# Output projection of a hybrid attention block: float16 hi/lo pairs with a scale in place of float32r pairs

## The chip, the core and the metric

The kernel runs on one core of a Trainium2 chip. The core has a matrix engine (TensorE; its weight loads are shown apart), three engines for elementwise work and reductions (VectorE, ScalarE, GpSimd), and a queue of its own for issuing transfers (SyncE); all run at the same time and wait for each other through semaphores. The time of a run is in microseconds on the device. The profile is of one execution and covers the span from its first to its last instruction.

## The reference

One layer of an encoder block over 1024 tokens of width 1024. One projection `h = x @ W_in` gives the columns of two groups of heads and of their gates; group A is neighbourhood attention over a 64 x 16 grid with a learned bias, group B is windowed grouped-query attention with rotary positions and a sink. What bears on the change is the end:

```
mixed = concat([y_a * silu(z_a), y_b * silu(z_b)], axis=-1)      # 1024 tokens x 1024
y     = mixed @ W_out                                            # 1024 x 1024
out   = LayerNorm(ALPHA * x + y, gain, bias)                     # ALPHA = 2 ** 0.25
```

All inputs and outputs are float32. A product of two float32 matrices is formed in this kernel from pairs: each operand is split into a part `hi` in a shorter type and the rest `lo`, and three products are added: hi x hi, hi x lo, lo x hi.

## The kernel before

All products are built of 128 x 128 stationary tiles and moving tiles of up to 512 columns. The stages follow one another, and overlap.

1. **V projection** (L430, to 61.7 us): x and the V columns of W_in in float32r pairs. Beside it the scale of x is found (`x_max`, `x_scale`), and x is loaded a second time and split into scaled float16 pairs (`x16_part`).
2. **Six first projections** (61.7 to 124.3 us): `project` (L334) for the first `NPRO = 6` names of `ORDER`: gate tiles zb0, z0, zb1, the keys and first queries of group B, and gate z1. A name is a tile of 128 columns of W_in and takes 48 matmuls of 512 columns in L355: two token halves, eight k-tiles, three products. W_in is split into float16 pairs after scaling with a power of two: `w_scan` or `sum_w` sums the absolute values of a tile, `w_scale` forms the total over the partitions with a matmul against `ones` (L207) and derives the scale. For the first six names a tile has a scale of its own; the other 15 share one, for which `sum_w` reads them all once in this stage, tile i at step 14 + 14 i; eight of them stay in SBUF, seven are loaded again later.
3. **Attention** (124.3 to about 374 us): 128 units. Each has a score product (L709, L710), row maximum and exponential, a split of the probabilities with a DMA transpose, the product with V (L774), and a transposition back (L794) with which the gate is multiplied in. Between the units' matmuls the other 15 projections are fed in, by a table of times (`FILL_AT`), and after them the first 60 output matmuls (`out_head`).
4. **Output projection** (`out_mms`, L899; 350.9 to 445.7 us): per token tile t and column half a, eight k-tiles e of three products each. `m_split` and `m_queue` make float32r pairs of the gated tiles (`mh`, `ml`), `wo_split` makes those of the 16 half tiles of W_out. Each finished half goes to `residual` (VectorE: ALPHA x + y, with statistics), and each finished token tile to `norm` and out.

What sets the order of the work: in stages 1 and 2 the instructions stand in each engine's queue as the program emits them (`tc.manual_schedule`). In stage 2 a counter `ran` goes up by one per projection matmul (`run_to`, L364), and work listed with `at(c, ...)` is emitted when it reaches c: this text calls c the step. Rotation and splitting of keys and queries are listed relative to their projection's end (`after=`). In stage 3, `enq` and `pop` put work of ScalarE, VectorE, GpSimd and SyncE into queues and take it out unit by unit. Stage 4 (`final`) is ordered by the framework's planner. Buffers are rings: a load into a buffer waits until the last reader of its old content is done, and everything behind that load in SyncE's queue waits with it. Projections write to two alternating banks (`bank("pj")`); a bank is taken again once it has been copied out.

## Time and profile before

| | us |
|---|---|
| median of 3 runs (lowest, highest) | 455.62 (455.61, 455.85) |
| profiled execution | 455.19 |
| its span, first to last instruction | 453.4 |
| TensorE busy | 443.6 |
| VectorE / ScalarE / GpSimd busy | 333.3 / 287.7 / 227.7 |
| mean granted TensorE clock | 0.995 |
| moved by DMA | 82.28 MB |

Times in rows of the profile count from the start of the span. In a row, PE is TensorE, PEld its weight loads, DVE VectorE, ACT ScalarE, POOL GpSimd and SP SyncE; `L355` is a line of the kernel, `out<-in` are the kernel's names of tiles, and the number after an x is a count. A matmul's own duration contains the time in which it runs through the array beside its neighbours, so the pace of a stream is the distance between starts, which the chain of work shows. An idle time is put down to the work that ended it.

### The profile page before, as it was taken

To read this page: it belongs to the slowest core of one execution; us is meant where nothing else is said; L and a number is where in the kernel's file an instruction comes from. 1 tells how busy PE (TensorE), PEld (TensorE's weight loads), DVE (VectorE), ACT (ScalarE), POOL (GpSimd) and SP (SyncE) were. 2 spreads that over 40 slices of the span, in tenths; PEclk is the share of its full clock that TensorE was granted. 3 is DMA by queue.
4 is the path that set the end of the run, shared out by engine and by line. 5 is a ranking of instruction groups with operands and counts; after the bars stand their busy time and mean duration, and the time that the engine had idled before them with its cause. 6 is when DMAs were issued, how large, how long until landed. Compare 5 with 4: busy or idle time off the path is not lost.

```text
span 453.4 us, 9438 instructions
## 1 busy us (share of the span) xinstructions
PE 443.6 (98%) x3260; PEld 295.2 (65%) x3260; DVE 333.3 (73%) x808; ACT 287.7 (63%) x664; POOL 227.7 (50%) x235
## 2 busy tenths in 40 slices
PE   8999999999999999999999999999999999999993
PEld 8999964444445565555555656555556788888882
DVE  5796956538987877896888878877878739099644
ACT  5648659776499877788777887686878825012100
POOL 0003944546848559688326766444773344007621
PEclk9999999999999999999999999999999999999998
DMA  8897277984657798599777989999999886004511
GB/s 263 275 328 259 78 256 248 322 307 167 209 114 150 157 174 158 113 140 170 162 170 159 167 173 214 195 147 200 218 189 234 159 249 267 1 19 147 187 55 57
DMA packets 134415, 82.28 MB, mean 181 GB/s; under 512 B 101344, under 2 KB 113504, under 8 KB 134112
## 3 DMA queue, kind: packets, MB, share of 16 engines
q1 hardware_dynamic: 133936, 81.26, 73.3%
q8 instruction: 25, 0.41, 0.4%
q10 hardware_dynamic: 432, 0.43, 0.4%
q14 instruction: 22, 0.18, 0.1%
HBM read 51.25 MB, written 9.96 MB: 135 GB/s over the span
## 4 chain that ended last, share of the span: by engine, by line
PE 88%; DVE 3%; issue 2%; POOL 2%; DMA 2%; ACT 2%; DVEq 0%; SPq 0%; POOLq 0%; ACTq 0%
PE ps_pj L355 42%; PE ps_s L899 9%; PE ps_s L430 6%; PE ps_t L774 6%; PE ps_pj L899 6%; PE ps_t L899 5%; PE ps_s L709 3%; PE ps_s L710 3%; PE ps_pj L430 3%; PE ps_t L430 3%; DMA bias<-in_bias 1%; PE ps_t L794 1%; DVE qs L240 1%; POOL ks L272 1%; ACT split L745 1%
## 5 line engine op out<-in xcount | busy, mean ns | idle before, releaser
L355 PE MATMUL ps_pj<-xf,wh 128*128 128x512 f16 x672 | 202.1, 379 | 0.9 <-DVE qs L240 0.6
L355 PE MATMUL ps_pj<-xf,wl 128*128 128x512 f16 x336 | 127.3, 379 | 0.0
L355 PEld LDWEIGHTS <-wh 128*128 128x128 f16 x672 | 63.5, 98 | 61.6 <-DVE ks L240 1.0
L735 ACT ACTIVATE ps_s<-sn,nm 128x385 f32<-128x385 f32 (+3 forms) x128 | 70.2, 549 | 33.0 <-DVE nm L719 31.8
L746 DVE SCALAR_TENSOR_TENSOR split<-ps_s,split 128x384 f16<-128x384 f32 (+2 forms) x128 | 65.6, 513 | 27.5 <-ACT split L745 26.0
L745 ACT ACTIVATE split<-ps_s 128x384 f16<-128x384 f32 (+2 forms) x128 | 57.4, 449 | 1.8
L355 PEld LDWEIGHTS <-wl 128*128 128x128 f16 x336 | 32.9, 98 | 37.4
L719 DVE CUSTOM_DVE_ANT_0 sn<-ps_s,bm,nsk 128x384 f32<-128x384 f32 (+1 forms) x64 | 40.8, 637 | 7.0 <-PE ps_s L710 6.4
L899 PE MATMUL ps_s<-wo,m 128*128 128x512 f32 (+1 forms) x192 | 43.3, 379 | 0.0
L719 DVE CUSTOM_DVE_ANT_0 sn<-ps_s,bias,sg 128x264 f32<-128x264 f32 (+1 forms) x64 | 35.0, 548 | 10.9 <-PE ps_s L710 3.1
L186 POOL TENSOR_SCALAR wr<-wr,wsc 128x512 f32<-128x512 f32 x26 | 20.6, 792 | 39.9 <-ACT wh L181 33.8
L709 PE MATMUL ps_s<-ks,qs 128*128 128x384 f16 (+4 forms) x128 | 39.3, 307 | 0.0
L710 PE MATMUL ps_s<-ks,qs 128*128 128x384 f16 (+4 forms) x128 | 39.2, 306 | 0.0
L681 POOL TENSOR_SCALAR bias<-bias,rsg 128x552 f32<-128x552 f32 (+1 forms) x24 | 19.2, 799 | 39.4 <-DMA bias<-in_bias 25.5
L899 PEld LDWEIGHTS ps_s<-wo,m 128*128 128x128 f32 x192 | 34.4, 188 | 7.0
L774 PEld LDWEIGHTS <-tr 128*128 128x128 f16 (+1 forms) x1104 | 36.5, 98 | 2.2 <-issue 0.3
L953 ACT ACTIVATE sd<-mv,eps 128x1 f32<-128x1 f32 x8 | 2.4, 294 | 49.9 <-DVE mv L951 45.8
L187 POOL TENSOR_TENSOR wl<-wr,wh 128x512 f16<-128x512 f32 x26 | 32.6, 1254 | 2.2
L272 POOL COPY ks<-ks 64x512 f16<-64x512 f16 x40 | 26.3, 665 | 10.3 <-DVE ks L240 5.4
L989 POOL TENSOR_TENSOR xr<-xr,gb 128x512 f32<-128x512 f32 x7 | 10.3, 1476 | 40.8 <-ACT xr L986 40.8
L430 PE MATMUL ps_s<-wvh,x 128*128 128x320 f32 x128 | 29.6, 311 | 0.0
L899 PE MATMUL ps_pj<-wo,m 128*128 128x512 f32 (+1 forms) x120 | 28.6, 376 | 0.0
(147 smaller groups left out, 827.4 us busy)
## 6 DMA issues: line engine op xcount, KB each, us to landing
xraw<-in_xT SPq DMA_DIRECT2D x31, 256.0 KB, 4.2
ws<-in_wt SPq DMA_DIRECT2D x15, 512.0 KB, 5.5
wr<-in_wt SPq DMA_DIRECT2D x26, 256.0 KB, 3.1
bias<-in_bias SPq DMA_DIRECT2D x16, 276.0 KB, 3.3
wor<-in_wo SPq DMA_DIRECT2D x16, 256.0 KB, 3.6
xr<-in_x SPq DMA_DIRECT2D x8, 512.0 KB, 6.7
out<-xr SPq DMA_DIRECT2D x14, 256.0 KB, 2.1
bias<-in_bias SPq DMA_DIRECT2D x8, 368.0 KB, 4.0
```

Source lines behind the costliest of these rows:

```text
L187: nc.gpsimd.tensor_sub(l, raw, h)
L272: nc.gpsimd.tensor_copy(t[o, sl], t[a, sl])
L355: nc.tensor.matmul(ps, a[:, k % 4, :], mv, start=(k == 0 and i == 0), stop=(k == KT - 1 and i == 2))
L430: nc.tensor.matmul(ps[:, :320], lh[t // 4, k][:, ts], rh[k][:, cs], start=(k == 0 and i == 0), stop=(k == KT - 1 and i == 2))
L709: nc.tensor.matmul(ps[:, :m], q, sl[0], start=True, stop=False)
L710: nc.tensor.matmul(ps[:, :m], q, sl[1], start=False, stop=True)
L719: nc.vector.tensor_tensor_reduce(sn[:, :m], ps[:, :m], bias_t, sg[:, c:c + 1], init, op0=ALU.add, op1=ALU.min, accum_out=nm)
L735: nc.scalar.activation(pt[:, :m], sn[:, :m], AF.Exp, bias=nm, scale=-1.0, accum_out=sm[:, k:k + 1])
L745: nc.scalar.activation(hl[:, :m, 0, :c], src, AF.Copy, scale=PSCALE)
L746: nc.vector.scalar_tensor_tensor(hl[:, :m, 1, :c], src, PSCALE, hl[:, :m, 0, :c], op0=ALU.mult, op1=ALU.subtract)
L774: nc.tensor.matmul(ps[:, HD * m:HD * m + HD], a, b_, start=(i == 0), stop=(i == len(mms) - 1))
L899: nc.tensor.matmul(ps, lh[:, ts], rh[:, cs], start=(e == EO[0] and i == 0), stop=(e == EO[-1] and i == 2))
```

## The change

The output projection's operands become float16 pairs (`mh`, `ml`, `wo_parts`), as the projections already are. Float16 has a small range, so both operands are scaled.

- The scale of the gated tiles needs a bound. `w_scan` and `sum_w` form column sums of absolute values for the eight gate tiles (`ZPRO` by position in `ORDER`, `ZSUM` by position among the later 15): a VectorE reduction to 128 values in place of one number (the gate tiles that ScalarE scanned before go to VectorE; the tiles 4 and 7, which VectorE scanned, go to ScalarE), a matmul against `ones` with 128 columns, and a maximum. The k dimension is summed with a stride of 128 elements. `sum_w` emits its matmul at its own step, 28, 84, 168 and 210.
- `m_scale` (step 226) combines these with the bounds of x and V into `msc` and multiplies it into the three columns (`zcol`) by which the gate multiplication already scales. The bounds themselves are kept, so a few in-place operations write elsewhere.
- W_out gets one scale, from a pass of its own: eight loads of 512 KB (`wo_sum_load`, the first three at step 70, each later one when a buffer comes free), a ScalarE sum for each (`wo_sum`, step 92 + 18 i), and `wo_scale` at step 240 (VectorE maximum, TensorE transpose, VectorE maximum and seven small steps in all).
- `wo_split` scales: the high part always on ScalarE with a scale; the low part on VectorE in one instruction, on GpSimd in two instead of one. `m_split` and `m_queue` change types only. A pair of W_out half tiles, and hi and lo of a gated tile, share a buffer.
- The factor of the result is taken out in `residual`, which multiplies by `oinv`; ALPHA is divided out of the sum, and put back through the gain (one ScalarE multiplication) and the scale of the square root.
- A smaller scratch area for the DMA queues is reserved.

```
+ZPRO = (0, 1, 2, 5)
+ZSUM = (1, 5, 11, 14)
...
     def w_scan(m):
+        if m // 2 in ZPRO:
+            nc.vector.tensor_reduce(cs[:, m % 2, :], raws[m].rearrange("p k c -> p c k"), axis=mybir.AxisListType.X,
+                                    op=ALU.add, apply_absolute_value=True)
+            return
         nc.scalar.activation(junk[:, :512], raws[m].rearrange("p k c -> p (k c)"), AF.Abs, accum_out=wm[:, m:m + 1])
 
     def w_scale(n):
...
-        nc.tensor.matmul(ps[:, :m], ones, wm.bitcast(BF16)[:, 2 * c + 1:2 * (c + m):2], start=True, stop=True)
-        nc.vector.tensor_reduce(g, ps[:, :m], axis=mybir.AxisListType.X, op=ALU.add if n < NPRO else ALU.max)
+        if n in ZPRO:
+            m = 128
+            for i in range(2):
+                nc.tensor.matmul(ps[:, :m], ones, cs[:, i, :].bitcast(BF16)[:, 1::2], start=(i == 0), stop=(i == 1))
+        else:
+            nc.tensor.matmul(ps[:, :m], ones, wm.bitcast(BF16)[:, 2 * c + 1:2 * (c + m):2], start=True, stop=True)
+        nc.vector.tensor_reduce(g, ps[:, :m], axis=mybir.AxisListType.X, op=ALU.max if n >= NPRO or n in ZPRO else ALU.add)
...
-            if i not in (1, 4, 7):
+            if i not in ZSUM:
                 nc.scalar.activation(junk[:, :1024], t, AF.Abs, accum_out=wm[:, c:c + 1])
             else:
-                nc.vector.tensor_reduce(wm[:, c:c + 1], t, axis=AXX, op=ALU.add, apply_absolute_value=True)
+                nc.vector.tensor_reduce(cs[:, 0, :], sums[i].rearrange("p h k c -> p c (h k)"), axis=AXX, op=ALU.add,
+                                        apply_absolute_value=True)
+                nc.vector.tensor_reduce(wm[:, c:c + 1], cs[:, 0, :], axis=AXX, op=ALU.add)
+                ps = bank("t")
+                nc.tensor.matmul(ps[:, :128], ones, cs[:, 0, :].bitcast(BF16)[:, 1::2], start=True, stop=True)
+                j = ZSUM.index(i)
+                nc.vector.tensor_reduce(zc[:, j:j + 1], ps[:, :128], axis=AXX, op=ALU.max)
             sum_load(i + 4)
...
+        def m_scale():
+            nc.vector.tensor_reduce(zg, zc, axis=AXX, op=ALU.max)
+            for n in ZPRO:
+                nc.vector.tensor_max(zg, zg, wg[:, n:n + 1])
+            nc.vector.tensor_scalar_max(zg, zg, 2.0 ** -30)
+            nc.vector.tensor_mul(zg, zg, gm)
+            nc.vector.tensor_mul(zg, zg, vg)
+            nc.vector.tensor_scalar_mul(zg, zg, 2.0 ** 13 / 60000.0)
+            nc.vector.reciprocal(msc, zg)
+            for i, t in enumerate((vsc, vscb[:, 0:1], vscb[:, 1:2])):
+                nc.vector.tensor_mul(zcol[:, i:i + 1], t, msc)
...
+        def wo_sum_load(i):
+            if i < KT:
+                wo_raws[i] = wp.tile([128, D], F32, tag="wos", name=f"wos{i}", bufs=3)
+                nc.sync.dma_start(wo_raws[i], wo[i])
+
+        def wo_sum(i):
+            nc.scalar.activation(junk[:, :D], wo_raws.pop(i), AF.Abs, accum_out=wom[:, i:i + 1])
+            wo_sum_load(i + 3)
+
+        def wo_scale():
+            nc.vector.tensor_reduce(wog, wom, axis=AXX, op=ALU.max)
+            ps = bank("t")
+            nc.tensor.transpose(ps[:, :128], wog.to_broadcast([128, 128]), identf)
+            nc.vector.tensor_reduce(wog, ps[:, :128], axis=AXX, op=ALU.max)
...
+        at(226, m_scale)
+        for i in range(3):
+            at(70, wo_sum_load, i)
+        for i in range(KT):
+            at(92 + 18 * i, wo_sum, i)
+        at(240, wo_scale)
...
     def m_alloc(e, pool):
+        if pool is big:
+            t = big_tile(f"m{e}", (128, 2, S), F16)
+        else:
+            t = pool.tile([128, 2, S], F16, tag="m", name=f"m{e}", bufs=4)
+        mh[e], ml[e] = t[:, 0, :], t[:, 1, :]
...
-            copy = nc.scalar.copy if hi_eng == "act" else nc.vector.tensor_copy
-            copy(wo_parts[n][0], wo_raw[n])
+            nc.scalar.activation(wo_parts[n][0], wo_raw[n], AF.Copy, scale=wos)
 
         def lo():
             h, l = wo_parts[n]
-            eng.tensor_sub(l, wo_raw.pop(n), h.bitcast(F32))
+            raw = wo_raw.pop(n)
+            if q == "dve":
+                nc.vector.scalar_tensor_tensor(l, raw, wos, h, op0=ALU.mult, op1=ALU.subtract)
+            else:
+                nc.gpsimd.tensor_scalar(raw, raw, wos, 1.0, op0=ALU.mult, op1=ALU.mult)
+                nc.gpsimd.tensor_sub(l, raw, h)
...
         gb, bb = gain_tile[0], zslot("bb")
+        nc.scalar.mul(gb, gb, ALPHA)
...
-                nc.vector.scalar_tensor_tensor(xv, xv, ALPHA, ps[:, o:o + w], op0=ALU.mult, op1=ALU.add)
+                nc.vector.scalar_tensor_tensor(xv, ps[:, o:o + w], oinv, xv, op0=ALU.mult, op1=ALU.add)
```

More of the change, by code (lines that the diff above doesn't have):

```diff
@@ L109, in hybrid_block @@
     sg = const.tile([128, 3], F32, name="sg")
+    cs = const.tile([128, 2, 128], F32, name="cs")
+    zc = const.tile([128, 4], F32, name="zc")
+    zg = const.tile([128, 1], F32, name="zg")
+    msc = const.tile([128, 1], F32, name="msc")
+    zcol = const.tile([128, 3], F32, name="zcol")
+    wom = const.tile([128, KT], F32, name="wom")
+    wog = const.tile([128, 1], F32, name="wog")
+    wos = const.tile([128, 1], F32, name="wos")
+    oinv = const.tile([128, 1], F32, name="oinv")
     rsg = const.tile([128, 1], F32, name="rsg")
@@ L206, in w_scale @@
         ps = bank("t")
-        nc.tensor.matmul(ps[:, :m], ones, wm.bitcast(BF16)[:, 2 * c + 1:2 * (c + m):2], start=True, stop=True)
-        nc.vector.tensor_reduce(g, ps[:, :m], axis=mybir.AxisListType.X, op=ALU.add if n < NPRO else ALU.max)
+        if n in ZPRO:
[5 more added lines that the diff above has]
+        nc.vector.tensor_reduce(g, ps[:, :m], axis=mybir.AxisListType.X, op=ALU.max if n >= NPRO or n in ZPRO else ALU.add)
         nc.vector.tensor_scalar_max(g, g, 2.0 ** -30)
-        nc.vector.tensor_scalar(g.bitcast(I32), g.bitcast(I32), 0x7F800000, None, op0=ALU.bitwise_and)
-        nc.vector.tensor_scalar(wsc[:, n:n + 1].bitcast(I32), g.bitcast(I32), 0x7F800000, None, op0=ALU.bitwise_xor)
-        nc.vector.tensor_scalar(v, g, xrs, 0.5, op0=ALU.mult, op1=ALU.mult)
+        nc.vector.tensor_scalar(v.bitcast(I32), g.bitcast(I32), 0x7F800000, None, op0=ALU.bitwise_and)
+        nc.vector.tensor_scalar(wsc[:, n:n + 1].bitcast(I32), v.bitcast(I32), 0x7F800000, None, op0=ALU.bitwise_xor)
+        nc.vector.tensor_scalar(v, v, xrs, 0.5, op0=ALU.mult, op1=ALU.mult)
         nk, nq = ORDER.index("kb"), ORDER.index("qb0")
@@ L324, in z_col @@
     def z_col(e):
-        return vsc if e in (4, 0, 5) else vscb[:, 0:1] if e == 1 else vscb[:, 1:2]
+        i = 0 if e in (4, 0, 5) else 1 if e == 1 else 2
+        return zcol[:, i:i + 1]
     groups = []
@@ L455, in x_scale @@
             nc.vector.tensor_scalar_max(gm, gm, 2.0 ** -16)
-            nc.vector.tensor_scalar(gm.bitcast(I32), gm.bitcast(I32), 0x7F800000, None, op0=ALU.bitwise_and)
-            nc.vector.tensor_scalar_mul(xrs, gm, 2.0 ** -14)
+            nc.vector.tensor_scalar(xrs.bitcast(I32), gm.bitcast(I32), 0x7F800000, None, op0=ALU.bitwise_and)
+            nc.vector.tensor_scalar_mul(xrs, xrs, 2.0 ** -14)
             nc.vector.reciprocal(xsc, xrs)
@@ L551, in hybrid_block @@
             v_max(t)
-        vg = vw.tile([128, 1], F32, name="vg")
+        vg = const.tile([128, 1], F32, name="vg")
         def v_scale():
@@ L559, in v_scale @@
             nc.vector.tensor_reduce(vg, ps[:, :128], axis=AXX, op=ALU.max)
-            nc.vector.tensor_scalar_max(vg, vg, 2.0 ** -100)
-            nc.vector.tensor_scalar(vg.bitcast(I32), vg.bitcast(I32), 0x7F800000, None, op0=ALU.bitwise_and)
-            nc.vector.tensor_scalar_mul(vsc, vg, 2.0 ** -14)
+            nc.vector.tensor_scalar_max(vg, vg, 2.0 ** -60)
+            nc.vector.tensor_scalar(vsc.bitcast(I32), vg.bitcast(I32), 0x7F800000, None, op0=ALU.bitwise_and)
+            nc.vector.tensor_scalar_mul(vsc, vsc, 2.0 ** -14)
             nc.vector.reciprocal(vrs, vsc)
@@ L601, in at @@
             events.setdefault(c, []).append(lambda: fn(*a))
-        at(16, v_scale)
+        def m_scale():
[9 more added lines that the diff above has]
+                nc.vector.tensor_mul(zcol[:, i:i + 1], t, msc)
+        wo_raws = {}
+        def wo_sum_load(i):
[10 more added lines that the diff above has]
+            nc.vector.tensor_reduce(wog, ps[:, :128], axis=AXX, op=ALU.max)
+            nc.vector.tensor_scalar_max(wog, wog, 2.0 ** -30)
+            nc.vector.tensor_scalar(wog.bitcast(I32), wog.bitcast(I32), 0x7F800000, None, op0=ALU.bitwise_and)
+            nc.vector.reciprocal(wos, wog)
+            nc.vector.tensor_scalar_mul(wos, wos, 2.0 ** 14)
+            nc.vector.tensor_scalar(oinv, zg, wog, 2.0 ** -14 / ALPHA, op0=ALU.mult, op1=ALU.mult)
+        at(16, v_scale)
+        at(226, m_scale)
[4 more added lines that the diff above has]
+        at(240, wo_scale)
         for t in range(9):
@@ L823, in m_alloc @@
     def m_alloc(e, pool):
-        for parts_ in (mh, ml):
-            if pool is big:
-                parts_[e] = big_tile(f"m{e}", (128, S))
-            else:
-                parts_[e] = pool.tile([128, S], F32R, tag="m", name=f"m{e}", bufs=8)
+        if pool is big:
[3 more added lines that the diff above has]
+        mh[e], ml[e] = t[:, 0, :], t[:, 1, :]
     def m_split(e, sl, hi, lo):
         hi(mh[e][:, sl], zt[e][:, sl])
-        lo(ml[e][:, sl], zt[e][:, sl], mh[e][:, sl].bitcast(F32))
+        lo(ml[e][:, sl], zt[e][:, sl], mh[e][:, sl])
     WO_SEQ = [(e, a) for a in range(2) for e in EO[:4]] + [(e, a) for e in EO[4:] for a in range(2)]
-    wo_parts = {}
+    wo_parts, wo_pair = {}, [None]
     wo_raw = {}
@@ L852, in hi @@
             if n < 8:
-                t = big_tile(f"wo{n}")
-            elif n < 13:
-                t = tiles["fp"].tile([128, 2, 512], F32R, tag="wo", name=f"wo{n}", bufs=5)
+                if n % 2 == 0:
+                    wo_pair[0] = big_tile(f"wo{n}", (128, 2, 2, 512), F16)
+                t = wo_pair[0][:, n % 2]
             else:
-                t = zp.tile([128, 2, 512], F32R, tag=("zc", "zd", "ze")[n - 13], name=f"wo{n}", bufs=1)
+                t = tiles["fp"].tile([128, 2, 512], F16, tag="wo", name=f"wo{n}", bufs=8)
             wo_parts[n] = [t[:, 0, :], t[:, 1, :]]
-            copy = nc.scalar.copy if hi_eng == "act" else nc.vector.tensor_copy
-            copy(wo_parts[n][0], wo_raw[n])
+            nc.scalar.activation(wo_parts[n][0], wo_raw[n], AF.Copy, scale=wos)
         def lo():
             h, l = wo_parts[n]
-            eng.tensor_sub(l, wo_raw.pop(n), h.bitcast(F32))
-        eng, q = (nc.vector, "dve") if n % 3 == 2 else (nc.gpsimd, "pool")
-        hi_eng = "act" if clock["step"] is not None or WO_SEQ[n][1] == 1 else "dve"
-        o = enq(hi_eng, hi, load_ops.get(("wo", n)))
+            raw = wo_raw.pop(n)
[4 more added lines that the diff above has]
+                nc.gpsimd.tensor_sub(l, raw, h)
+        q = "dve" if n % 3 == 2 else "pool"
+        o = enq("act", hi, load_ops.get(("wo", n)))
         o = enq(q, lo, o)
@@ L881, in m_queue @@
             m_ops[e].append(enq("pool", lambda h=h: nc.gpsimd.tensor_sub(
-                ml[e][:, h], zt[e][:, h], mh[e][:, h].bitcast(F32)), o))
+                ml[e][:, h], zt[e][:, h], mh[e][:, h]), o))
     LT, LP = LTT, LPP
@@ L952, in row_stats @@
             sd = fp.tile([128, 1], F32, tag="sd", name="sd")
-            nc.scalar.activation(sd, mv[:, 1:2], AF.Sqrt, bias=eps)
+            nc.scalar.activation(sd, mv[:, 1:2], AF.Sqrt, bias=eps, scale=ALPHA ** 2)
             return mv, sd
@@ L1160 @@
     host = _host(inputs)
-    nc = bacc.Bacc("TRN2", target_bir_lowering=False, num_devices=1)
+    nc = bacc.Bacc("TRN2", target_bir_lowering=False, num_devices=1, dynamic_dma_scratch_size=1024)
     arrays, args = {}, []
```

## The prediction, made before the changed kernel had run

> **What bounds the kernel now.** I read the page's first part, then the windows by stage, TensorE's waits, the chain, and last the queues of VectorE and SyncE around the places that the change touches.

> ```profile
> PE 443.6 (98%) x3260; PEld 295.2 (65%) x3260; DVE 333.3 (73%) x808; ACT 287.7 (63%) x664; POOL 227.7 (50%) x235
> ```
> ```profile
> 61.90:124.30 62.40, 62.40 (x296) 28.49 (x295) 40.90 (x88) 45.03 (x81) 37.73 (x38) 1.00 0.76 258
> 124.30:200.00 75.70, 75.70 (x643) 42.64 (x642) 60.60 (x176) 62.07 (x157) 50.84 (x51) 1.00 0.73 146
> ...
> 380.00:399.00 19.00, 19.00 (x84) 15.47 (x83) 7.51 (x13) 0.00 (x0) 0.23 (x1) 1.00 0.10 34
> 399.00:445.70 46.70, 46.66 (x226) 38.91 (x225) 33.59 (x67) 7.55 (x14) 19.57 (x14) 1.00 0.29 102
> ```
> ```profile
> PE ps_t L389 <- DVE warm L386: 1.0, 1, 1.0
> PE ps_pj L355 <- DVE qs L240: 0.6, 1, 0.6
> PE ps_pj L355 <- DVE ks L240: 0.4, 1, 0.4
> PE ps_pj L430 <- ACT wvh L414: 0.2, 1, 0.2
> ```
> A window's columns are its limits, its length, then busy time of TensorE, its weight loads, VectorE, ScalarE and GpSimd, clock, DMA share, GB/s. TensorE is busy without a gap from the six first projections to the last output matmul, and in the whole run waits 2.2 us (the sum of the last fence's first numbers). So a nanosecond off a matmul is a nanosecond off the time, and a wait put before a matmul is paid in full: no later idle time of TensorE gives it back.

> ```profile
> 71.04 0.00 PE ps_t L207
> 71.05 10.38 PE ps_pj L355 x48
> ...
> 91.82 10.38 PE ps_pj L355 x48
> ...
> 102.20 7.14 PE ps_pj L355 x33
> 109.34 0.01 PE ps_t L207
> ...
> 401.33 5.53 PE ps_pj L899 x24
> ...
> 442.80 2.87 PE ps_pj L899 x24
> ```
> This chain (start, length, what) gives the paces and a calendar. Steps of the hand-written list are counted in projection matmuls. L207 of step 42 lies at 71.05, so step 138 is at 91.82, step 186 at 102.20, step 219 at 109.35; at 10.38/48 = 0.2163 us a step, TensorE comes to step 28 at 68.0, 84 at 80.1, 168 at 98.3, 210 at 107.4 and 240 at 113.9.

> **The gain: float16 output matmuls.**
> ```profile
> L899 PE MATMUL ps_s<-wo,m x192: 277/389/475, 359.4 to 442.5; 128*128 128x512 f32 x168, 128*128 128x256 f32 x24
> L899 PE MATMUL ps_pj<-wo,m x120: 276/389/525, 350.9 to 445.4; 128*128 128x512 f32 x96, 128*128 128x256 f32 x24
> L899 PE MATMUL ps_t<-wo,m x96: 387/391/477, 373.5 to 423.0; 128*128 128x512 f32 x96
> ```
> 360 matmuls of 512 columns and 48 of 256 change type. At 512 columns float32r goes at 5.53/24 = 230.4 ns, float16 (L355) at 216.3: 14.1 ns less, 360 times, 5.1 us. At 256 columns float32r goes at 119.6; no row has float16 there, so between 10 and 14 ns less, 0.5 to 0.7. Together **-5.7 us**. All of them lie in stretches where TensorE has no gap.

> **What TensorE gets besides.** Eight 128-column sums for the gate tiles of the first six replace four tiny ones, four more come in the later scan, and one transpose. A quarter of a 512-column pace is 0.05 us; the tiny ones cost 0.01. 12 x 0.05 - 4 x 0.01, and 0.11 for the transpose (as for the one that exists, one step between two pieces of the chain): **+0.7 us**, at most 1.4 if each costs 0.11.

> **The waits.** This is the main part. The old scan of the later weight tiles had no TensorE instruction until step 219. Now `sum_w` of the four gate tiles puts one at steps 28, 84, 168 and 210, each behind a VectorE reduction issued at the same step, and `wo_scale` puts a transpose at step 240 behind a VectorE reduction, behind `m_scale`. The order there is written by hand, so each engine runs it as it stands; a matmul that waits holds all projections behind it, and everyone who waits for these. What counts is where VectorE stands when TensorE comes by.

> ```profile
> 66.62 1.21 DVE L597 TENSOR_REDUCE wm<-ws 128x1 f32<-128x1024 f32 x1
> ...
> 79.55 1.21 DVE L597 TENSOR_REDUCE wm<-ws 128x1 f32<-128x1024 f32 x1
> 80.67 0.87 DVE L571 SCALAR_TENSOR_TENSOR vt<-v,vrs,vt 128x640 f16<-128x640 f32 x1
> 81.58 0.23 DVE L572 COPY vb<-vt 128x256 f16<-128x256 f16 x1
> ...
> 84.58 1.21 DVE L597 TENSOR_REDUCE wm<-ws 128x1 f32<-128x1024 f32 x1
> ...
> 108.59 1.81 DVE L242 TENSOR_TENSOR ks<-rp_raw,ks 64x512 f16<-64x512 f32 x2
> 110.33 0.01 DVE L289 LOAD_MASK_SELECT rp_sw<-rp_raw  x1
> ...
> 116.92 0.01 DVE L289 LOAD_MASK_SELECT rp_sw<-rp_raw  x1
> ```
> ```profile
> 104.20:110.33 6.13, 6.13 (x31) 2.81 (x30) 6.03 (x8) 6.05 (x11) 4.67 (x5) 1.00 0.36 123
> 110.33:116.92 6.59, 6.59 (x32) 3.00 (x31) 6.31 (x20) 3.05 (x6) 6.17 (x7) 1.00 0.50 165
> ```
> - Step 28: VectorE starts this tile at 66.62. Ahead of it now stands the scan of weight half 5, moved from ScalarE, half the elements of the 66.62 row and so 0.6 us. 66.62 + 0.6 + 1.21 = 68.45 against 68.0: **0.5**.
> - Step 84: the reduction at 79.55 goes to ScalarE, so the V part at 80.67 starts there and takes 1.1 with its copy (the two rows); the new sum ends at 79.55 + 1.1 + 1.21 = 81.86. TensorE would be there at 80.1, or 80.6 with the first wait: 1.3 to 1.8, **1.4**, since part of VectorE's work moves with TensorE and part not.
> - Step 210: the program puts this sum between the two rows that end and start at 110.33 (key halves of step 199, queries' shuffle of step 217). VectorE is busy 6.03 of the 6.13 us before, since step 192's rotation, and both move together with any earlier delay. The sum ends at 111.55, TensorE stands there at 107.4: **4.2**.
> - Step 240: after that wait TensorE comes to step 216 at 112.95; ScalarE copies in half a microsecond, VectorE's shuffle starts at about 113.5 (it waits; its own extra reduction ends before). From there VectorE has the work of 110.33 to 116.92, 6.6 us, then `m_scale`'s 13 column operations at 0.19 from start to start (below), 2.5, then the maximum, 0.2: 122.8. TensorE is at step 240 at 118.1: **4.7**.
> - Step 168: here data decide. SyncE fetches tile 11 with two others at 92.79, once the weight load ahead of it is released.

> ```profile
> 92.39 0.34 SPq L170 DMA_DIRECT2D wr<-in_wt  x1
> 92.79 1.45 SPq L587 DMA_DIRECT2D ws<-in_wt  x3
> ```
> ```profile
> DMA to landing us min/median/max: 3.7/5.5/7.7
> ```
> ```profile
> 86.00:90.00 4.00, 4.00 (x20) 1.84 (x19) 0.00 (x0) 2.71 (x7) 4.00 (x7) 1.00 1.11 368
> ```
> At 92.79 with 3.7 to 7.7 us it lands at 96.5 to 100.5; plus 1.21. TensorE, 1.9 late by then, is there at 100.2: a wait of 0 to 1.5 as things stand. The change adds eight loads of W_out, 512 KB each, from step 70 on, 4.2 MB at 370 GB/s or 11 us of traffic where the DMA engines are full (share 1.11 in the last row), and in SyncE's queue each later one waits until ScalarE has read an earlier one, with the weight and scan loads queued behind it. ScalarE waits for the first at step 92, and GpSimd's weight split, SyncE's release, after it. I add 1 to 3 us: 0 to 4, taken at **2.4**.

> Sum of the waits: 0.5 + 1.4 + 2.4 + 4.2 + 4.7 = **13.2 us**.

> The strided sums are priced like the reductions of as many contiguous elements. No row reads with a stride of 512 bytes, so between once and twice that: step 28 +1.8, and 1.2 at 84, 168 and 210, 5.4 us at most. I take none, the one row being that of the same operation and size.

> [...]

> **What I cost at nothing, and its cover.**
> ```profile
> 38.30 0.29 DVE L454 TENSOR_REDUCE gm<-ps_t 128x1 f32<-128x128 f32 x1 [2.15 <-PE ps_t L453]
> ...
> 65.79 0.15 DVE L560 TENSOR_SCALAR vg<-vg 128x1 f32<-128x1 f32 x1
> 65.98 0.15 DVE L561 TENSOR_SCALAR vg<-vg 128x1 int32<-128x1 int32 x1
> ```
> ```profile
> 98.84 1.05 ACT L595 ACTIVATE junk<-ws 128x1024 bf16<-128x1024 f32 x1
> ```
> Four weight scans on VectorE ahead of the 38.30 row take 4 x 0.6 of its 2.15 us idle: 0.3 late, and the float16 x parts that follow have some 6 us before step 0. ScalarE's eight `wo_sum` (1.05 plus a readout, 9 us; 3.6 go to VectorE) find 17 us idle in the first window above; without that, evacuations come late, and a projection bank gives 5 us. W_out's splits get dearer (a scaling multiply on GpSimd, 0.7; all highs on ScalarE, 0.7 each) and the gain multiply is new on ScalarE, 1.1: cover is the 380 to 399 window, ScalarE 0.00 and GpSimd 0.23 busy; the first users might wait 0 to 1 us. Residual and statistics keep their instructions, and the float16 tiles need half the buffers.

> **Sum.** The profiled execution took 455.19 (span 453.4), 0.43 under the median. 455.19 - 5.7 + 0.7 + 13.2 = 463.4; with 0.43, **463.8 us**. Within 0.2% (0.9 us) nothing can be told from no change.

> **Rivals.**
> *Faster: VectorE is there first.* At step 112 (86.2) VectorE's reduction began at 84.58, ahead of TensorE; were it so at 168, 210 and 240 too, 11.3 us go: 452.5. The point is 5.0 us for the five waits together. Against it stand the two busy rows from 104.20 to 116.92. 0.08; within 0.2%, 0.02.
> *Smaller waits*, 7 to 10 us, the data of step 168 in time and VectorE less slowed by GpSimd: 457.5 to 461. 0.09.
> *Strided sums at twice the price:* 463.8 + 5.4 = 469.2. 0.13.
> *The clock drops in the long waits.*
> ```profile
> 448.70:449.20 0.50, 0.00 (x0) 0.00 (x0) 0.50 (x1) 0.00 (x0) 0.42 (x2) 0.83 0.00 0
> 449.20:449.70 0.50, 0.00 (x0) 0.00 (x0) 0.50 (x2) 0.00 (x0) 0.50 (x1) 0.50 0.00 0
> ```
> ```profile
> 0.99 3.06 PE L389 MATMUL ps_t<-warm 128*128 128x128 f16 x27 [0.99 <-DVE warm L386]
> ```
> The last matmul ended at 445.67; 0.83 over half a microsecond puts the fall to 0.50 at 449.03, after 3.4 us idle. Steps 210 and 240 wait longer. The first 27 matmuls went at 113 ns where 54 is the full pace, so slow work lasts 3.1 us or somewhat more and costs half of that, about 1.8 per fall: 465.6 with one, 467.4 with both. 0.17. [...]
> *The matmuls get no faster* (230 ns stay): 469.5. Against it stands the float16 pace of the chain, 216 ns over 48 at a time. 0.03.
> The forecast itself, 461 to 466.5: 0.48.

> The range leaves out the faster cases and the end of the strided one: 457 to 470. Faster 0.08, same 0.02, slower 0.90.

> **What would show it.** In the changed kernel's trace: 24 output matmuls of 512 columns in 5.2 us in place of 5.53; TensorE rows waiting for VectorE at the four sums and the transpose of `wo_scale`, 13 us together, the last two longest; step 288 (124.3 now) some 14 us later; the stretch from there to the first output matmul as long as now; clock below 1.00 near 115 or 125 only in the clock case. I am wrong if those waits sum to under 5 us, or if TensorE lost its time after step 288.

## The result, and the profile after

The changed kernel takes 475.07 us (median of 6 runs, 473.53 to 478.68) against 455.62 (455.08 to 455.93): a ratio of 1.0438, 95% interval 1.0402 to 1.0475. It is slower, as forecast, but by 19.5 us where 8.2 were forecast, and outside the range. The profiled execution took 475.26 us, with a span of 473.4.

The first view again is what TensorE waits for; its columns are the sum, how often, and the longest, in us.

```profile
PE ps_t L622 <- DVE cs L618: 12.6, 4, 5.0
PE ps_t L656 <- DVE wog L654: 4.0, 1, 4.0
```

The rows are the four column sums and the transpose of `wo_scale`. Each one by itself is in TensorE's timeline (start, length, what; in brackets the idle time ahead and who ended it), steps 28, 84, 168, 210 and 240:

```profile
70.02 0.27 PE L622 MATMUL ps_t<-cs,ones 128*128 128x128 bf16 x1 [2.27 <-DVE cs L618]
86.43 0.22 PE L622 MATMUL ps_t<-cs,ones 128*128 128x128 bf16 x1 [2.43 <-DVE cs L618]
109.37 0.22 PE L622 MATMUL ps_t<-cs,ones 128*128 128x128 bf16 x1 [2.87 <-DVE cs L618]
123.76 0.27 PE L622 MATMUL ps_t<-cs,ones 128*128 128x128 bf16 x1 [4.99 <-DVE cs L618]
136.47 0.47 PE L656 MATMUL ps_t<-identf,wog 128*128 128x128 f32 x1 [4.01 <-DVE wog L654]
```

Together 16.6 us. The windows, with the columns of the prediction, show a second loss: the granted clock. The first row is the whole second stage, from its first projection matmul to the first score matmul; the others cut out the waits of steps 210 and 240.

```profile
61.42:149.45 88.03, 71.46 (x303) 30.99 (x302) 55.34 (x124) 49.74 (x87) 34.88 (x38) 0.88 0.69 242
...
120.00:124.00 4.00, 0.24 (x2) 0.21 (x2) 3.90 (x5) 0.24 (x1) 3.16 (x5) 0.63 0.80 311
124.00:128.00 4.00, 4.00 (x13) 1.41 (x11) 1.05 (x4) 1.37 (x2) 0.93 (x1) 0.52 0.38 123
...
132.00:136.00 4.00, 0.46 (x3) 0.00 (x0) 3.59 (x13) 3.16 (x5) 3.42 (x4) 0.83 0.10 39
136.00:140.00 4.00, 3.53 (x9) 1.42 (x10) 3.26 (x14) 0.00 (x0) 2.00 (x3) 0.50 0.39 117
```

From 124 to 128 TensorE is busy without a gap and runs 13 matmuls; at the 0.216 us of the chain before it is 18 or 19 in that time. Narrow windows around the change of clock date the falls (0.83 over 0.4 us that began at 1.00 and ended at 0.50 is a fall about two thirds of the way through).

```profile
69.80:70.20 0.40, 0.18 (x2) 0.18 (x2) 0.37 (x2) 0.40 (x1) 0.00 (x0) 0.51 1.03 399
73.00:73.40 0.40, 0.40 (x3) 0.19 (x2) 0.00 (x0) 0.00 (x0) 0.00 (x0) 0.72 1.05 387
86.60:87.00 0.40, 0.40 (x4) 0.14 (x2) 0.40 (x3) 0.00 (x0) 0.00 (x0) 0.85 0.93 379
90.20:90.60 0.40, 0.40 (x3) 0.13 (x2) 0.40 (x1) 0.35 (x1) 0.00 (x0) 0.89 0.92 338
109.00:109.40 0.40, 0.03 (x1) 0.03 (x1) 0.37 (x2) 0.00 (x0) 0.00 (x0) 1.00 1.03 369
121.00:121.40 0.40, 0.00 (x0) 0.00 (x0) 0.37 (x2) 0.00 (x0) 0.29 (x1) 0.51 1.21 410
127.60:128.00 0.40, 0.40 (x4) 0.19 (x3) 0.39 (x1) 0.40 (x1) 0.00 (x0) 0.70 0.29 123
134.40:134.80 0.40, 0.00 (x0) 0.00 (x0) 0.37 (x2) 0.40 (x1) 0.40 (x1) 0.83 0.00 0
141.40:141.80 0.40, 0.40 (x3) 0.23 (x2) 0.37 (x2) 0.00 (x0) 0.00 (x0) 0.89 0.00 0
```

The clock is at one half from 69.8 to 73.2, 86.9 to 90.3, 121.0 to 127.8 and 134.7 to 141.5. TensorE works for 3.2, 3.4, 4.1 and 5.0 us of these, 15.7 in all, at 0.43 us from one matmul of 512 columns to the next where it is 0.216 at a clock of 1.00: 7.8 us lost. The third wait, 2.87 us before 109.37, left the clock at 1.00.

The gain lies after that stage. A row of the kernel before that the prediction does not show, then the same and the last piece of the chain of the changed kernel:

```profile
124.10 0.27 PE L709 MATMUL ps_s<-ks,qs 128*128 128x256 f16 x1
```
```profile
149.45 0.27 PE L776 MATMUL ps_s<-ks,qs 128*128 128x256 f16 x1
```
```profile
424.14 5.18 PE ps_pj L969 x24
...
463.02 2.63 PE ps_pj L969 x24
```

From the first score matmul to the last output matmul it takes 465.65 - 149.45 = 316.2 us, before 445.67 - 124.10 = 321.6: 5.4 less. 24 output matmuls take 5.18 us (before 5.53), at 256 columns 2.63 (2.87). The second stage grew from 62.4 to 88.0 us, by 25.6: 16.6 of waits, 7.8 of half clock, 0.7 of TensorE's own added work (from one start to the next a column sum takes 0.06, a pair of them 0.12 and the transpose 0.27), 0.5 left over. 25.6 - 5.4 is the 20.1 us between the two profiled executions, within 0.1.

### The profile page after: what moved, and what is told of

Same layout as the page of the kernel before. It is cut to its first block, busy times and chain, and to the rows that moved or that the text cites. A ratio compares the mean times of both kernels' runs of the same rounds, so it can differ in the third digit from the quotient of the medians.

```text
span 473.4 us, 9527 instructions
## 1 busy us (share of the span) xinstructions
PE 446.7 (94%) x3269; PEld 265.3 (56%) x3269; DVE 349.7 (74%) x841; ACT 294.5 (62%) x667; POOL 232.1 (49%) x246
## 4 chain that ended last, share of the span: by engine, by line
PE 73%; DVE 7%; issue 6%; POOL 5%; DMA 4%; SPq 2%; ACT 2%; DVEq 0%; POOLq 0%; ACTq 0%
PE ps_pj L376 34%; PE ps_s L451 6%; PE ps_t L841 6%; PE ps_s L969 5%; PE ps_pj L969 4%; PE ps_s L776 3%; PE ps_s L777 3%; PE ps_pj L451 3%; PE ps_t L451 3%; DMA ws<-in_wt 3%; PE ps_t L969 3%; POOL wl L198 2%; DMA xr<-in_x 2%; PE ps_t L861 1%; POOL wor L934 1%
## 5 line engine op out<-in xcount | busy, mean ns | idle before, releaser
L376 PE MATMUL ps_pj<-xf,wh 128*128 128x512 f16 x672 | 208.0, 388 | 0.9 <-DVE qs L260 0.6
L376 PE MATMUL ps_pj<-xf,wl 128*128 128x512 f16 x336 | 130.4, 388 | 0.0
L376 PEld LDWEIGHTS <-wh 128*128 128x128 f16 x672 | 64.8, 100 | 77.4 <-issue 19.5
L969 PEld LDWEIGHTS <-m 128*128 128x128 f16 x408 | 39.6, 98 | 41.9 <-issue 0.8
L197 POOL TENSOR_SCALAR wr<-wr,wsc 128x512 f32<-128x512 f32 x26 | 18.5, 713 | 59.4 <-ACT wh L192 53.1
L969 PE MATMUL ps_s<-wo,m 128*128 128x512 f16 (+1 forms) x192 | 40.8, 366 | 0.0
L969 PE MATMUL ps_pj<-wo,m 128*128 128x512 f16 (+1 forms) x120 | 26.5, 358 | 0.0
L499 POOL TENSOR_SCALAR xraw<-xraw,xsc 128x512 f32<-128x512 f32 x5 | 5.3, 1060 | 42.2 <-ACT xf L497 42.2
L802 ACT ACTIVATION_READ_ACCUMULATOR ps_s<-sn,nm 128x1 f32 x128 | 24.1, 188 | 0.0
```

Source lines behind the costliest of these rows:

```text
L376: nc.tensor.matmul(ps, a[:, k % 4, :], mv, start=(k == 0 and i == 0), stop=(k == KT - 1 and i == 2))
L802: nc.scalar.activation(pt[:, :m], sn[:, :m], AF.Exp, bias=nm, scale=-1.0, accum_out=sm[:, k:k + 1])
L969: nc.tensor.matmul(ps, lh[:, ts], rh[:, cs], start=(e == EO[0] and i == 0), stop=(e == EO[-1] and i == 2))
```

## The experiments

Ratios are to runs of the kernel before on the same chip (medians 455.1 to 455.5), with their 95% interval.

**The clock: spare work in the waits.**

```
+                for _ in range((10, 11, 13, 22)[ZSUM.index(i)]):
+                    nc.tensor.matmul(ps, x16h[0, 0][:, :128], x16h[0, 0], start=True, stop=True)
                 nc.tensor.matmul(ps[:, :128], ones, cs[:, 0, :].bitcast(BF16)[:, 1::2], start=True, stop=True)
...
+            for _ in range(18):
+                nc.tensor.matmul(ps, x16h[0, 0][:, :128], x16h[0, 0], start=True, stop=True)
             nc.tensor.transpose(ps[:, :128], wog.to_broadcast([128, 128]), identf)
```

> Before each of the five waiting TensorE instructions stand 10, 11, 13, 22 and 18 spare float16 matmuls of 512 columns into the same bank, a little less than the wait that they stand in (2.3, 2.4, 2.9, 5.0 and 4.0 us at 216 ns each); nothing else is changed, and the output is the same. Theory: the granted clock falls to one half because TensorE is idle in these waits, and this costs about 7.3 us beside the 17.4 us of waiting. With the spare work the clock stays at 1.00, and 475.1 becomes about 468, less of a gain if a wait grows because TensorE comes to it earlier. Rival: the waits themselves are the whole loss, VectorE and the data setting the pace, so that a faster TensorE only waits longer: 474 to 476.

470.74 us, ratio 1.0326 [1.0295, 1.0357], mean clock 0.997 where it was 0.974. So TensorE does more work and the kernel is 4.3 us faster: here the clock is a loss of its own, and the rival falls. It is not 7.8 us, because TensorE now comes earlier to VectorE's results. The waits still there in its profile:

```profile
PE ps_t L624 <- DVE cs L618: 2.6, 2, 2.3
PE ps_t L660 <- DVE wog L656: 0.8, 1, 0.8
```

With 74 spare matmuls of 0.216 us, 16.0, TensorE spends 19.4 us where it spent 16.6 waiting: 2.8 of the 7.8 are lost again. That leaves 5.0, of which 4.3 are measured; the 0.7 between them stay open.

**The stride.**

```
-            nc.vector.tensor_reduce(cs[:, m % 2, :], raws[m].rearrange("p k c -> p c k"), axis=mybir.AxisListType.X,
+            nc.vector.tensor_reduce(cs[:, m % 2, :], raws[m].rearrange("p k (a b) -> p (k a) b", b=4), axis=mybir.AxisListType.X,
...
-                nc.vector.tensor_reduce(cs[:, 0, :], sums[i].rearrange("p h k c -> p c (h k)"), axis=AXX, op=ALU.add,
+                nc.vector.tensor_reduce(cs[:, 0, :], sums[i].rearrange("p h k (a b) -> p (h k a) b", b=8), axis=AXX, op=ALU.add,
```

> The eight weight scans and four gate sums on VectorE write 128 sums each as before, but every sum is now over elements that lie next to each other (4 or 8 in a row) instead of 512 bytes apart; the sums are then not those of the columns, and the bound is another. Theory: the stride makes them dear, 1.92 and 1.04 us where the same number of contiguous elements took 1.21 and 0.68 in the kernel before; the durations go back to these, the waits lose about 3.5 us, and the time is about 470, less by up to 4 more if a fall of the clock goes with them. Rival: it is the 128 results instead of one that make them dear: 1.92 and 1.04 stay, and the time is 475.

The groups of instructions (count, then busy time and ns of one) of the changed kernel and of this one:

```profile
L213 DVE TENSOR_REDUCE cs<-wr 128x128 f32<-128x512 f32 x8 | 8.2, 1051 | 0.0
L618 DVE TENSOR_REDUCE cs<-ws 128x128 f32<-128x1024 f32 x4 | 7.7, 1914 | 6.1 <-DMA ws<-in_wt 6.1
```
```profile
L213 DVE TENSOR_REDUCE cs<-wr 128x128 f32<-128x512 f32 x8 | 5.2, 676 | 0.0
L618 DVE TENSOR_REDUCE cs<-ws 128x128 f32<-128x1024 f32 x4 | 4.9, 1214 | 6.8 <-DMA ws<-in_wt 6.8
```

And TensorE's waits in this one:

```profile
PE ps_t L622 <- DVE cs L618: 9.7, 4, 4.3
PE ps_t L656 <- DVE wog L654: 3.8, 1, 3.8
```

1914 and 1051 ns become 1214 and 676: the stride costs a factor of 1.58 and 1.55, and 128 results cost the same as one (the row at 66.62 in the prediction has 1.21 for as many elements). The five waits go from 16.6 to 13.5 us. The time, 473.01 us (1.0375 [1.0333, 1.0417]), falls by only 2.1 of the 5 expected. Between the two profiled executions it is 3.0 (475.26 and 472.24): 3.1 us of waits go, and the time lost at half clock goes from 7.8 to about 5.4 us (it is at one half only from 117.6 to 124.4 and from 131.2 to 138.1), but other waits of TensorE grow by 1.8, the longest of them 1.2 us behind a DMA transpose in the attention. VectorE still waits 6.8 us for the tiles of these sums (the last number of its row); a faster sum does not bring the data earlier.

**The gain by itself.**

```
-ZPRO = (0, 1, 2, 5)
-ZSUM = (1, 5, 11, 14)
+ZPRO = ()
+ZSUM = (1, 4, 7)
...
-        at(226, m_scale)
...
-        at(240, wo_scale)
+        nc.gpsimd.memset(wos, 2.0 ** 10)
+        nc.gpsimd.memset(oinv, 2.0 ** -10 / ALPHA)
```

> The float16 output projection alone: the scales of the gated outputs and of W_out are constants, so that the column sums, their TensorE instructions, m_scale, the pass over W_out and wo_scale are left out, and the scan of the weights stands as in the kernel before. Theory: the step from float32r to float16 is worth 5.7 us, and the dearer splits of W_out cost 0 to 0.5: 455.6 becomes 450 to 450.5. Rival: the dearer splits (a multiply on GpSimd, all high parts on ScalarE) give part of the gain back or the matmuls gain less: 452 or more.

449.82 us, ratio 0.987 [0.9838, 0.9901]: 5.6 less than before. The term of 5.7 holds, and the dearer W_out splits cost nothing that can be seen. All the 25 us between this and the changed kernel hang on how the scales are found.

**TensorE's part later.**

```
-        at(226, m_scale)
+        for j in range(2):
+            at((60, 130)[j], z_max, j)
...
+        if i == 3:
+            z_max(2)
+            z_max(3)
+        if i == 4:
+            m_scale()
...
+        if i == 8:
+            wo_scale()
```

> All the work of the change is kept, but TensorE's part of it stands later: each gate sum has a buffer of its own, its product with the ones comes at steps 60 and 130 and, for the last two, at the fourth attention unit, m_scale at the fifth and the transpose of wo_scale at the ninth. VectorE's reductions and ScalarE's pass over W_out stay where they are. Theory: what the change loses is where TensorE waits for VectorE, so no wait over 0.5 us is left before the attention, the clock stays at 1.00, and the time is 452 to 456. Rival: the added load of VectorE and of the DMA engines is itself the loss, and the projections or the first attention units come late whatever TensorE waits for: 460 or more.

463.30 us (1.0163 [1.0122, 1.0204]). 11.8 us come back, but the number lies in the rival's range, and "no wait over 0.5 us" does not hold. None of the five instructions waits any more, but three scales that TensorE formed at these steps before the change do now, and the clock is at one half from 118.6 to 125.4:

```profile
95.31 0.16 PE L228 MATMUL ps_t<-wm,ones 128*128 128x2 bf16 x1 [1.34 <-ACT junk L217]
...
107.72 0.22 PE L226 MATMUL ps_t<-cs,ones 128*128 128x128 bf16 x1 [1.81 <-DVE cs L214]
119.93 0.19 PE L228 MATMUL ps_t<-wm,ones 128*128 128x15 bf16 x1 [4.87 <-DVE wm L622]
```

L228 at 119.93 is the common scale of the later projections (step 219), which was there before and needs all the sums. With the gate sum of step 210 on VectorE, one of its inputs now stands behind the stretch of rotations in which VectorE was busy 6.03 of 6.13 us. So a second reason lies under the first: what feeds an old instruction had been moved to an engine that comes to it later. The next two kernels take the two suspects apart.

**The pass over W_out left out of that kernel.**

```
-            at(70, wo_sum_load, i)
-        for i in range(KT):
-            at(92 + 18 * i, wo_sum, i)
+        nc.gpsimd.memset(wom, 16.0)
```

> The late kernel with the pass over W_out left out (its sums are a constant), so that the eight loads of 512 KB and ScalarE's eight sums are gone; all else as in the late kernel (463.3 us, in which TensorE still waited 4.9 us at the step-219 scale behind VectorE's gate sum of step 210, 1.8 us at the step-186 scale behind VectorE's late gate sum of step 168, and 1.3 us at the step-138 scale behind ScalarE). Theory: the W_out pass fills the DMA queue of SyncE, and the 1.8 and the 1.3 us come from it; they go, the 4.9 us and the fall of the clock in it stay: about 460. Rival: the waits come from VectorE's load alone and not from the loads of W_out: 463.

457.47 us (1.0056 [1.0034, 1.0078]): by the medians 5.8 less than with the pass, by the ratios 4.9. The 1.34 and the 1.81 us are gone (0.2 is left of the second), the 4.8 stays:

```profile
PE ps_t L228 <- DVE wm L622: 4.8, 1, 4.8
...
PE ps_t L226 <- DVE cs L214: 0.2, 1, 0.2
```

For the waits that is what the theory says; the time fell by more than its 3 us. The profiled execution is the slowest of the ten (455.70 to 460.92), and only 2.5 us faster than the one of the late kernel. There the sum comes out: 3.0 of waits and 1.3 of an earlier second stage (it begins at 63.65 and 62.34) are won, 1.5 are lost again in one wait of TensorE behind a DMA transpose in the attention, and 0.3 at half clock. The 1.3 lie ahead of that stage, and so ahead of the pass, which begins at step 70 of it. Why the medians differ by 5.8 these runs do not show in full.

**Gate sums 11 and 14 back on ScalarE, their column sums in the attention.**

```
-            if i not in ZSUM:
+            if i not in ZSUM[:2]:
...
+        if i == 3:
+            z_cols(2)
+        if i == 7:
+            z_max(2)
+            z_cols(3)
...
+        if i == 13:
+            m_scale()
```

> The late kernel with the pass over W_out where the change has it, but the scans of the gate tiles 11 and 14 on ScalarE as the other tiles have it, and their column sums on VectorE only at the fourth and eighth attention unit (m_scale at the fourteenth, the transpose of wo_scale at the seventeenth). Theory: the 4.9 us at step 219 is VectorE's queue at step 210 and the fall of the clock comes with it; both go, and the 1.8 us of step 186 with them; the wait of ScalarE for W_out stays: 454 to 456. Rival: the loads of W_out make all later data late whoever reads them, and ScalarE's scans of tiles 11 and 14 are waited for instead: 459 or more.

461.33 us (1.0125 [1.01, 1.0151]). The wait behind VectorE at step 219 is gone, as the theory has it, but the number is in the rival's range, for two reasons. ScalarE, which also has the W_out sums, is late at both scales, and in the attention `m_scale`, thirteen column operations in a row on VectorE, holds a score matmul:

```profile
95.07 0.16 PE L228 MATMUL ps_t<-wm,ones 128*128 128x2 bf16 x1 [2.32 <-ACT junk L217]
116.41 0.17 PE L228 MATMUL ps_t<-wm,ones 128*128 128x15 bf16 x1 [1.87 <-ACT junk L617]
...
161.22 0.37 PE L782 MATMUL ps_s<-ks,qs 128*128 128x256 f16 x1 [3.50 <-DVE split L819]
```

The three make 7.7 us, the clock is at one half behind the first and the last of them (95.8 to 99.2 and 160.7 to 164.1, about 3.1 us lost), and TensorE's own work is 0.7: together the 11.5 us that this kernel stands above the gain by itself.

**Both, with the W_out pass at the seam of the stages.**

```
+            nc.vector.tensor_reduce(zg, wz[:, 0:8], axis=AXX, op=ALU.max)
+            nc.vector.tensor_scalar(zg, zg, 2.0 ** -30, 2.0 ** 13 / 60000.0, op0=ALU.max, op1=ALU.mult)
+            nc.vector.scalar_tensor_tensor(zg, zg, gm, vg, op0=ALU.mult, op1=ALU.mult)
             nc.vector.reciprocal(msc, zg)
...
+            nc.vector.tensor_scalar_mul(zcol, vs3, msc)
...
-            at(70, wo_sum_load, i)
...
+            at(242, wo_sum_load, i)
...
+            at(266 + 10 * i, wo_sum, i)
...
```

> The late kernel with both: gate tiles 11 and 14 as in the last one, and the pass over W_out moved to steps 242 to 288 and the first ten attention units, where the DMA engines were 5 to 35% busy; besides, VectorE's first four weight scans stand behind the scale of x, each scan has a buffer of its own, and m_scale is 5 instructions instead of 13. The whole computation is there. Theory: nothing of the change is then ahead of TensorE; the gain of 5.7 us is left less 0.7 us of TensorE's own work and 0 to 2 us of late evacuations in the attention: 450.5 to 453, faster than the kernel before. Rival: VectorE and ScalarE are full in the first attention units (over 85% busy in the kernel before), and the added work there is paid in full: 455 or more.

462.90 us (1.0158 [1.0114, 1.0201]), a miss. The second stage is as short as before (62.55 to 125.25 us), and then most of it is lost in one place: ScalarE stands still for the first tile of W_out, the casts of the queries behind it are late, and TensorE waits 5.5 us and then works at half clock until 142.8, about 2.8 us more. Two further waits behind the same line of VectorE (0.75 us at 154.06, 0.83 at 162.34) and one of 1.2 us behind a DMA transpose come later.

```profile
126.92 1.06 ACT L652 ACTIVATE junk<-wos 128x1024 bf16<-128x1024 f32 x1 [5.96 <-DMA wos<-in_wo]
127.97 1.24 ACT L257 CAST qs<-rp_raw 64x512 f16<-64x512 f32 x2
...
137.24 0.48 PE L777 MATMUL ps_s<-ks,qs 128*128 128x384 f16 x1 [5.46 <-DVE split L814]
```

SyncE's queue shows why:

```profile
122.57 0.33 SPq L182 DMA_DIRECT2D wr<-in_wt  x1
122.95 1.38 SPq L649 DMA_DIRECT2D wos<-in_wo  x3
```

The W_out loads went out only at 122.95 us, behind a weight load that waited for its buffer until GpSimd had split the old content (to 122.55), and ScalarE had the first 4 us later. That the DMA engines had room (a share of 0.20 from 112 to 116 us, 0.71 from 120 to 124) did not give the load its turn in the queue any earlier.

**The W_out pass early.**

```
+            if i == 2:
+                for n in range(3):
+                    wo_sum_load(n)
...
+            if i == 5:
+                for n in range(3):
+                    wo_sum(n)
...
+            if i == 7:
+                wo_sum(3)
+                wo_sum(4)
```

> The last kernel with one thing changed: the pass over W_out stands in the values' stage, its first three loads at about 50 us and five of the eight sums on ScalarE before step 0, the rest at steps 16, 52 and 60; between 52 and 62 us ScalarE was busy 4.2 of 10 us and the DMA engines moved 77 GB/s there. Theory: what cost the last kernel its time is one wait of ScalarE, 6.0 us for the first W_out tile at step 266, with the casts of the queries behind it; without it the first score matmul comes as early as in the last kernel (about 62.7 us after step 0), TensorE does not wait there, and the time is 450.5 to 453, faster than the kernel before. Rival: the gate sums and m_scale on VectorE in the first attention units hold TensorE (the last kernel had waits of 0.8 us at 154 and 162 us too): 455 or more; or the loads delay the weights and step 0: 455 or more with step 0 after 64 us.

455.07 us, 452.92 to 459.06 in ten runs, ratio 1.0009 [0.998, 1.0038]: level with the kernel before. (ScalarE's 4.2 us in the text above are of 50 to 62 us; from 52 to 62 it was busy 2.5.) The wait at the seam is gone, and one of 2.38 us is left; in the profiled execution the clock did not fall behind it (the matmuls that follow start 0.216 us apart):

```profile
84.36 0.16 PE L228 MATMUL ps_t<-wm,ones 128*128 128x2 bf16 x1 [2.38 <-ACT junk L217]
```

The five runs with a mean clock of 0.994 to 0.997 took 452.9 to 454.5 us, the four with 0.988 to 0.992 took 456.7 to 459.1 (one with 0.993: 455.65). So clock and time go together, but one or two falls, at the 1.68 us of the kernel of gaps below, are 1.7 to 3.4 us, and the spread is 6; where the slow ones lost the rest is not shown, since only a fast one has a trace.

**The W_out pass spread.**

```
-            if i == 7:
-                wo_sum(3)
-                wo_sum(4)
...
-        for i, c in ((5, 16), (6, 52), (7, 60)):
+        for i, c in ((3, 144), (4, 168), (5, 222), (6, 246), (7, 270)):
```

> The last kernel with one thing changed: only three of ScalarE's eight sums of the pass over W_out stand before step 0; the others come at steps 144, 168, 222, 246 and 270, where ScalarE had idle times of 1 to 3.5 us, and the last two loads at step 200. Theory: the last kernel's one wait of 2.4 us (step 138's scale behind ScalarE, which five sums of W_out between 62 and 79 us had made late), and its spread of 452.9 to 459.1 us, come from these sums; both go, and the time is 450.5 to 452.5, about 1% faster than the kernel before, the gain of 5.7 less TensorE's own 0.7 and some rest. Rival: the rest of the added work in the second stage, VectorE's gate sums and weight scans, makes another engine late there, and a wait over 1 us stays: 453 to 456.

451.54 us (450.83 to 452.97), ratio 0.9924 [0.9909, 0.9939]: 0.8% less than the kernel before, with the interval clear of 1, and with all of the change's computation. The six runs lie within 2.2 us. Its longest wait of TensorE beyond the start's is that of the queries, which the kernel before has too; the one at step 138 is 0.5 us:

```profile
PE ps_pj L377 <- DVE qs L261: 0.6, 1, 0.6
PE ps_t L228 <- ACT junk L217: 0.5, 1, 0.5
```

It stands 1.7 us above the gain by itself by the medians, 2.5 by the ratios; 0.7 of that is TensorE's own work.

**Gaps, and the clock behind them.** A kernel of gaps, whose operands are zeros:

```
...
+                for i in range(BLOCK):
+                    nc.tensor.matmul(ps[n % 2], lhs[n % 2], rhs, start=True, stop=True)
+                nc.vector.tensor_copy(pad[:, :128], ps[n % 2][:, :128])
+                for i in range(g):
+                    nc.vector.tensor_scalar_mul(pad, pad, 1.0)
+                n += 1
+                nc.vector.tensor_copy(lhs[n % 2], pad[:, :128])
```

> A kernel of its own that leaves the computation out (it copies x to the output): TensorE runs blocks of 71 float16 matmuls of 512 columns (15.4 us each), and between two blocks it waits for 1 to 16 short VectorE instructions, four gaps of each length, so that it is idle from about 1 to about 5 us. It asks what idle time makes the granted clock fall. [...]

This kernel ran once. A block of 71 matmuls takes 15.50 us at full clock. Blocks behind gaps of 1.63, 1.96, 2.29 and 2.94 us in TensorE's timeline:

```profile
204.92 15.50 PE L83 MATMUL ps<-rhs,lhs 128*128 128x512 f16 x71 [1.63 <-DVE lhs L88]
222.38 17.18 PE L83 MATMUL ps<-rhs,lhs 128*128 128x512 f16 x71 [1.96 <-DVE lhs L88]
241.52 15.50 PE L83 MATMUL ps<-rhs,lhs 128*128 128x512 f16 x71 [1.96 <-DVE lhs L88]
...
313.70 15.50 PE L83 MATMUL ps<-rhs,lhs 128*128 128x512 f16 x71 [2.29 <-DVE lhs L88]
331.49 17.18 PE L83 MATMUL ps<-rhs,lhs 128*128 128x512 f16 x71 [2.29 <-DVE lhs L88]
...
445.23 17.18 PE L83 MATMUL ps<-rhs,lhs 128*128 128x512 f16 x71 [2.94 <-DVE lhs L88]
```

In this run the clock never fell at gaps up to 1.63 us (12 gaps), at those of 1.96 once in four, of 2.29 and 2.62 twice in four, of 2.94 each time, of 3.27 three times in four, from 3.93 us on each time (12 gaps). So 3.4 us of idle time were not needed. Dated in windows of 0.4 us along the whole span, the 24 falls lie on one grid of 3.413 us, within 0.2 us, over 628 us. Counted between the lines of that grid, no interval at full clock with 1.8 us of idle time or less was followed by a fall, each one with 2.1 or more was, and of the few between all but one, with 2.03. Half clock lasted one interval (17 times) or two (7 times, all at gaps from 3.93 us on): one where the next interval had 0.78 us of idle time or less, two where it had 1.01 or more. One interval of steady work at half clock cost 1.68 us (17.18 against 15.50). Each of these intervals holds idle time from one gap; whether several short gaps in one add up was not tested.

The same grid fits the changed kernel: its falls at 86.9, 121.0 and 134.7 us lie 5, 15 and 19 times 3.413 us after the one at 69.8. Counted so, the wait of step 28 has 2.06 us in one interval, and the clock fell; the longer wait of step 168, 2.87 us, is cut by a line at 107.36 us into 0.9 and 2.0, and it did not.

## Why the prediction failed

*Right.* The gain (5.7; measured 5.4 in the profile and 5.6 by itself). Where TensorE waits: at exactly the five places named, behind VectorE, the last two longest. TensorE's own added work. No loss after the first score matmul. The items costed at nothing: the splits of W_out and the gain multiply show no cost in the kernel with the gain alone.

*The term that failed first: the clock, valued at nothing.* The forecast had a rival for it, at 0.17, and worked out 465.6 with one fall and 467.4 with both. Two of its steps were wrong. It took the one fall that the trace of before shows, 3.4 us after the last matmul, for the idle time needed; in the changed kernel the clock fell 2.1 to 2.2 us into the waits of steps 28, 210 and 240, and 0.4 us behind the wait of 2.43 us at step 84. By its reading only steps 210 and 240 could fall. It also took 1.8 us for a fall, from slow work of 3.1 us or somewhat more; steps 28 and 84 had 3.4 us of half clock each, steps 210 and 240 6.8. Lost: 7.8 us in the profile, of which 4.3 came back when the waits were filled.

*The second: the size of the waits*, 13.2 against 16.6. Step by step, forecast and measured: 0.5 and 2.27, 1.4 and 2.43, 2.4 and 2.87, 4.2 and 4.99, 4.7 and 4.01. The strided sums were priced as contiguous ones; they take 1.58 times as long (1914 ns for 1214). With contiguous sums the waits were 13.5 us, close to the 13.2 of the forecast, but partly by luck: the clock still fell twice, and place by place they are 0.46, 1.73, 3.18, 4.30 and 3.76. At step 28 the data were late too. VectorE's row and SyncE's first loads of the changed kernel, then those loads in the kernel before and in the one of the experiments that put the four weight scans behind the scale of x:

```profile
61.83 1.93 SPq L608 DMA_DIRECT2D ws<-in_wt  x4
...
68.06 1.91 DVE L618 TENSOR_REDUCE cs<-ws 128x128 f32<-128x1024 f32 x1 [0.67 <-DMA ws<-in_wt]
```
```profile
58.90 1.93 SPq L587 DMA_DIRECT2D ws<-in_wt  x4
```
```profile
59.66 1.93 SPq L609 DMA_DIRECT2D ws<-in_wt  x4
```

The four scans ahead of the scale of x take 4.0 us, where the forecast had 2.4, and its last reduction comes at 41.02 us in place of 38.30. The loads behind it come 2.9 us later, where the forecast had 0.3 at no price; with the scans behind the scale, 0.8. Step 0 itself is not late (its first matmul starts at 61.42, before at 61.69).

475.07 - 463.8 is 11.3: 7.8 and 3.4 make up 11.2; the 0.5 us left over in the second stage and the 0.3 missing from the gain are nearly made up for by where the profiled executions lie, 0.4 under the median before and 0.2 over it after.

*What the forecast did not see at all*, because the five waits hid it: with these gone, the common scale at step 219 waits 4.9 us for the gate sum that the change gave to VectorE, and the W_out pass makes ScalarE and the later tiles late. The forecast counted the W_out traffic as 1 to 3 us of one wait; without the pass, the kernel with the late TensorE part was 5 to 6 us faster by the medians and ratios, of which the traces show 3.0.

## What to carry to other kernels

A new instruction on the engine that sets the time costs what it waits for (16.6 us here), not what it takes (0.7): emit it where its inputs have long been there, and then look who waits next, for moving one wait away twice laid bare another here. A wait can cost more than its length: in the changed kernel four of the five, of 2.27 to 4.99 us, had TensorE at half clock in them or behind them, 7.8 us more, and one of 2.87 us did not. So read the granted clock beside the waits. A pass that is free by the busy shares still needs a place where its data are early and nothing stands behind it in the queue of its engine: at the seam, ScalarE stood still for 5.96 us for W_out, and TensorE behind it for 5.46.
